# RG-LRU gates with the split halves stacked in rows, and a later start of the weight splits

## The chip, the cores and the metric

The kernel runs on one core of a Trainium2 chip. A core has a matrix engine (TensorE, PE in the profile), a vector engine (VectorE, DVE), a scalar engine (ScalarE, ACT), GpSimd (POOL), and SyncE (SP), whose queue issues the transfers. PE writes its products to banks of PSUM; ACT and DVE read them from there. All work in SBUF, a memory of 128 partitions (rows). The metric is the device time of one execution in microseconds; the median of three runs of the kernel before is 1309.77 us.

## The reference

One step of a two-layer encoder over 512 prompt tokens and 32 sample tokens, 544 columns in all, with 1024 features. Each layer projects its input to the parts of three branches: attention, retention, and a gated linear recurrence (RG-LRU). The branches are merged through gates, projected out, and normalised. What matters here is the third branch, 512 features wide:

```
xc = conv_b + sum(xpad[:, j:j + t] * conv_w[j] for j in range(CONV_W))
xb = xc.reshape(b, t, N_BLOCKS_C, BLOCK_C)
r = sigmoid(einsum('btni,nij->btnj', xb, w_gate_a) + b_gate_a)
ig = sigmoid(einsum('btni,nij->btnj', xb, w_gate_x) + b_gate_x)
log_a = -LRU_C * r * softplus(-lru_lambda);  a = exp(log_a)
bx = sqrt(-expm1(2.0 * log_a)) * ig * xc
```

then h[t] = a[t] h[t-1] + bx[t]. Both gate matrices are block diagonal: 8 blocks of 64 x 64.

## The kernel before

Features lie in partitions, 128 to a tile, tokens in columns. Every weight matrix is cut into blocks of 128 x 128 in the order of their use, eight to a chunk of 512 KB. A chunk is loaded by SP into one of three `raw` buffers. For products of nearly full precision each operand is split into a high part (rounded to the format fp32r, which PE multiplies in one pass) and a low part (the rest): for weights ACT casts the high part (L209) and DVE subtracts it to get the low part (L210), four blocks at a time, two in the first chunk. `hilo` (L261 to L263) does the same with activations. `block` (L254) multiplies one weight block in three products, high by high, high by low and low by high, each in two column ranges of 288 and 256: six instructions.

`layer_units()` lists a layer's work as units, each with one output tile: eight `pl` units of two blocks (the per-layer embedding, whose inputs are split by `ple_split`), then `xr`, `va`, `qa`, `ka` and so on, mostly of eight blocks. A unit accumulates in one of two `mm` buffers; afterwards `evac` copies the result out, for `pl` with an ACT copy (L931), for `xr` with two (L888, L889).

The order on each engine is the order in which the program writes the instructions down, under a manual schedule. `tick()` runs before each weight block. It first calls `stream()`, which splits weights until they are LEAD = 8 blocks ahead of the block in use, and asks for the next chunk when a chunk's second half is split. It then advances the waiting jobs, generators that give back after how many ticks they want to go on; PACE has these numbers. So a job's instructions stand at fixed places between PE's blocks, and each engine works its queue strictly in turn.

At the start PE runs WARM = 16 products of zeros (`busy`), `stream(2)` splits the first four blocks, `ple_split(0)` splits the first inputs, and the job `x_job` splits the residual stream from tick 5 on, one of eight tiles every two ticks.

The gates are the job `lru_tile(t)`, one for each of four feature tiles, added when `xr` unit t is out. ACT and DVE form the convolution `xc` over 547 columns (512 prompt tokens, 3 of convolution history, 32 sample tokens; L504, L506). After a pause the high and low part are made over 128 partitions. After another, and once for each of the two gates: a 128 x 128 weight block that holds two 64 x 64 blocks on its diagonal, zeros elsewhere, is multiplied in three products (high by high, high by low, low by high), in two overlapping column ranges of 274, into one of two `sc` banks and the one `pv` bank (L516). Three sigmoids with bias write the result to `lru_r` or `lru_i` (L519 to L521), leaving out the three history columns. Three ticks later comes the second gate, then two multiplies on POOL (L523, L524). The tiles 1 and 2 overlap in time, so their groups of products alternate. After the last tile `lru_job` computes the recurrence (exp, tanh, sqrt, scans).

The gate weights lie in a `held` buffer, eight blocks a layer (`wg`): four for one gate, four for the other.

Of the kernel before, what the change touches and what calls it, by code (L numbers as in the profile page):

```python
# [18 lines left out]
N = NP + NS  # L19
# [47 lines left out]
HELD = (6, 2)  # L67
WARM = 16

# [19 lines left out]
P_SC, P_SL = 52, 64  # L89
P_S0 = 68  # L90
NPAR = P_S0 + 256

# [31 lines left out]
def encoder(ctx: ExitStack, tc, xT, pT, W, RB, KC, VC, PAR, CST, LGB, o_y, o_k, o_v, o_rp, o_rs, o_cv, o_lr):  # L124
# [48 lines left out]
    def tick():  # L173
        clock[0] += 1
        stream()
        for j in list(jobs):
            while j[1] <= clock[0]:
                d = next(j[0], None)
                if d is None:
                    jobs.remove(j)  # L180
                    break
                j[1] = clock[0] + d
# [78 lines left out]
    def hilo(h, lo, src):  # L261
        S.copy(h, src)  # L262
        V.tensor_tensor(lo, src, h.bitcast(F32), SUB)  # L263
# [18 lines left out]
    def ple_split(l):  # L282
        pr, p2 = ple_in[l]
        for k in range(2):
            hilo(p2[:, k], p2[:, 2 + k], pr[:, k])

# [34 lines left out]
    def layer(l, env, nxt):  # L321
# [176 lines left out]
        def lru_tile(t):  # L498
            if t == 0:
                env["lru"] = [sl("lru_r"), sl("lru_i"), sl("lru_a")]  # L500
            R, I, _ = env["lru"]
            xrp = env["xrp"]
            xc = tmp("xc", (128, W547))
            S.activation(xc, xrp[:, t, 0:W547], AF.Identity, scale=pcol(P_CW, t), bias=pcol(P_CB, t))  # L504
            for j in range(1, 4):
                V.scalar_tensor_tensor(xc, xrp[:, t, j:j + W547], pcol(P_CW + 4 * j, t), xc, MUL, ADD)  # L506
            yield PACE["lt1"]
            xch, xcl = (tp_.tile([128, W547], F32R, tag="tmp", name="xch") for _ in range(2))
            hilo(xch, xcl, xc)
            yield PACE["lt2"]  # L510
            for g in range(2):
                w, lo = ([parts[(l * NB + AT["wg"] + g * 4 + t) // 4][i][:, t] for i in range(2)])
                ps = psum("sc"), psum("pv")
                for i, (wg, x) in enumerate(((w, xch), (w, xcl), (lo, xch))):
                    for p_, c0 in ((ps[0], 0), (ps[1], W547 - 274)):
                        T.matmul(p_[:, :274], lhsT=wg, rhs=x[:, c0:c0 + 274], start=i == 0, stop=i == 2)  # L516
                d = (I if g else R)[:, t]
                b_ = pcol(P_BX if g else P_BA, t)
                S.activation(d[:, :274], ps[0][:, :274], AF.Sigmoid, bias=b_)  # L519
                S.activation(d[:, 274:NP], ps[1][:, 1:NP - 273], AF.Sigmoid, bias=b_)  # L520
                S.activation(d[:, NP:], ps[1][:, 274 - NS:274], AF.Sigmoid, bias=b_)  # L521
                yield PACE["lt3"]
            G.tensor_tensor(I[:, t, :NP], I[:, t, :NP], xc[:, :NP], MUL)  # L523
            G.tensor_tensor(I[:, t, NP:], I[:, t, NP:], xc[:, NP + 3:], MUL)  # L524
            if t == 3:
                env["gates"] = True
                add(lru_job())

        def lru_job():
            R, I, A = env["lru"]  # L530

            for t in range(4):
                S.activation(A[:, t], R[:, t], AF.Exp, scale=sp[:, 1, l, t:t + 1])
                S.activation(R[:, t], R[:, t], AF.Tanh, scale=sp[:, 0, l, t:t + 1])
                yield PACE["lru0"]
            y = I
            for t in range(4):
# [8 lines left out]
            for t in range(4):  # L546
                G.tensor_tensor(R[:, t], R[:, t], I[:, t], MUL)
                yield PACE["lru3"]
                V.tensor_tensor_scan(y[:, t, :NP], A[:, t, :NP], R[:, t, :NP], 0.0, MUL, ADD)
                V.tensor_tensor_scan(y[:, t, NP:], A[:, t, NP:], R[:, t, NP:], pcol(P_SL, t), MUL, ADD)  # L550
            yield 2
# [487 lines left out]
    with tc.manual_schedule():  # L1039
        envs = [{} for _ in range(L + 1)]  # L1040
        stream(2)
        ple_split(0)
# [86 lines left out]
```

## Time and profile before

| | before |
|---|---|
| median of three runs | 1309.77 us (1309.71 to 1310.03) |
| the profiled execution | 1309.81 us, of which the span of the trace is 1308.0 us |
| instructions | 25456, of which PE 10744 products |
| transfers | 125.90 MB, mean 96 GB/s |
| granted TensorE clock | 0.997 |

In the page, a group's line has the source line, the engine, the operation, output and input by the program's names, their shapes, and how many there were; then busy time, mean duration in ns, and the idle time of the engine before them with its cause. A row of the timeline has the start, the length, engine, line, operation, names, shapes and count; in brackets stands idle time before it and who ended it. `sc`, `pv`, `tp` and `mm` are PSUM banks. Ends of products are modelled: products overlap in the pipeline, and their lengths don't add up to time.

### The profile page before, as it was taken

The page shows a single profiled execution, that of the slowest core. Times are in us where ns is not written, and L with a number is a line of the kernel's source. Part 1 is how long each engine was busy: PE and PEld are TensorE (multiplying, and loading weights), DVE is VectorE, ACT ScalarE, POOL GpSimd, SP SyncE. Part 2 cuts the span into 40 slices and gives each one's busy share as a digit, 9 for nine tenths or more (in the row PEclk, how much of TensorE's full clock was granted, in tenths as well). Part 3 has the DMA queues.
Part 4 walks back from the last instruction along what each step waited for, and adds up shares of the span by engine and source line. Part 5 has one row for each costly group of instructions (what it writes and reads, how often), then busy time and mean ns, then how long its engine had stood idle before and what let it go on. Part 6 is the DMA issues. An engine that isn't in the chain of part 4 may idle for free.

```text
span 1308.0 us, 25456 instructions
## 1 busy us (share of the span) xinstructions
PE 1291.7 (99%) x10744; PEld 1263.5 (97%) x10744; DVE 717.3 (55%) x1271; ACT 546.1 (42%) x1065; POOL 177.0 (14%) x158
## 2 busy tenths in 40 slices
PE   9999999999999999999999999999999999999996
PEld 9999999999999999999989998999999999999996
DVE  5666662573753453465584756626637444434567
ACT  6665544323632232333277655443235322332231
POOL 0210120410101201000032201224001011010000
PEclk9999999999999999999999999999999999999998
DMA  7233522231222222224112335222222222222231
GB/s 282 66 131 98 171 69 80 85 105 50 85 93 82 97 68 94 97 97 146 65 49 66 131 99 166 74 83 82 89 66 81 95 83 86 92 81 97 81 113 69
DMA packets 43457, 125.90 MB, mean 96 GB/s; under 512 B 9360, under 2 KB 11664, under 8 KB 42576
## 3 DMA queue, kind: packets, MB, share of 16 engines
q1 hardware_dynamic: 43344, 124.29, 28.8%
q8 instruction: 84, 1.38, 0.4%
q14 instruction: 29, 0.24, 0.1%
HBM read 112.57 MB, written 7.24 MB: 92 GB/s over the span
## 4 chain that ended last, share of the span: by engine, by line
PE 95%; DVE 3%; DMA 1%; ACT 1%; issue 0%; SPq 0%; POOL 0%; DVEq 0%
PE mm L254 84%; PE pv L432 2%; PE sc L402 2%; PE tp L418 1%; PE tp L330 1%; DMA raw<-in_W 1%; PE sc L661 1%; PE pv L684 1%; PE pv L516 0%; DVE r L813 0%; PE sc L516 0%; DVE xl L263 0%; PE sc L744 0%; PE sc L597 0%; PE pv L679 0%
## 5 line engine op out<-in xcount | busy, mean ns | idle before, releaser
L254 PE MATMUL mm<-xh,wh 128*128 128x288 f32 x2144 | 455.5, 294 | 0.4 <-ACT xrp L889 0.4
L254 PE MATMUL mm<-xh,wl 128*128 128x288 f32 x2144 | 444.1, 288 | 0.0
L254 PE MATMUL mm<-xl,wh 128*128 128x288 f32 x2144 | 442.7, 288 | 0.0
L210 DVE TENSOR_TENSOR wl<-raw,wh 128x512 fp32r<-128x512 f32 (+1 forms) x354 | 261.4, 756 | 283.8 <-ACT wh L209 279.9
L254 PEld LDWEIGHTS mm<-xh,wh 128*128 128x128 f32 x2144 | 328.3, 189 | 10.7 <-issue 7.4
L254 PEld LDWEIGHTS mm<-xl,wh 128*128 128x128 f32 x2144 | 328.8, 188 | 0.0
L254 PEld LDWEIGHTS mm<-xh,wl 128*128 128x128 f32 x2144 | 328.5, 188 | 0.2 <-DVE wl L210 0.2
L209 ACT CAST wh<-raw 128x512 fp32r<-128x512 f32 (+1 forms) x354 | 208.3, 614 | 36.9 <-PE mm L254 30.8
L911 ACT ACTIVATE sg<-mm 128x544 f32<-128x544 f32 x48 | 30.1, 626 | 154.1 <-PE mm L254 154.1
L923 POOL TENSOR_TENSOR m<-m,sg 128x544 f32<-128x544 f32 x30 | 46.8, 1560 | 316.6 <-DVE sg L921 316.6
L355 ACT ACTIVATE sx<-sx,sst 128x128 f32<-128x128 f32 (+4 forms) x68 | 38.0, 559 | 70.1 <-DVE sst L353 66.0
L254 PE MATMUL mm<-xh,held 128*128 128x288 f32 (+1 forms) x320 | 64.0, 291 | 0.3 <-ACT ple L931 0.3
L254 PE MATMUL mm<-ml,wh 128*128 128x288 f32 (+1 forms) x256 | 52.9, 288 | 0.0
L254 PE MATMUL mm<-mh,wl 128*128 128x288 f32 (+1 forms) x256 | 52.6, 286 | 0.0
L254 PE MATMUL mm<-mh,wh 128*128 128x288 f32 (+1 forms) x256 | 52.5, 286 | 0.0
L254 PEld LDWEIGHTS mm<-xh,held 128*128 128x128 f32 x320 | 51.3, 188 | 0.6 <-ACT ple L931 0.5
L254 PE MATMUL mm<-xl,held 128*128 128x288 f32 (+1 forms) x160 | 46.4, 290 | 0.5 <-DVE xl L263 0.5
L262 ACT CAST xh<-r 128x544 fp32r<-128x544 f32 (+2 forms) x32 | 17.0, 532 | 67.8 <-DVE r L938 63.6
L921 DVE TENSOR_TENSOR sg<-mm,sg 128x544 f32<-128x544 f32 x32 | 23.2, 725 | 36.7 <-PE mm L254 36.7
L565 POOL TENSOR_TENSOR swap<-swap,cst 128x544 f32<-128x544 f32 x16 | 25.3, 1580 | 109.8 <-DMA swap<-QB 68.1
L902 ACT ACTIVATE z<-mm 128x544 f32<-128x544 f32 x24 | 15.0, 626 | 59.2 <-PE mm L254 59.1
L254 PEld LDWEIGHTS mm<-mh,wl 128*128 128x128 f32 x256 | 39.3, 188 | 0.0
(251 smaller groups left out, 1791.9 us busy)
## 6 DMA issues: line engine op xcount, KB each, us to landing
raw<-in_W SPq DMA_DIRECT2D x189, 512.0 KB, 3.3
bias<-in_RB SPq DMA_DIRECT2D x16, 256.0 KB, 4.1
x<-in_xT SPq DMA_DIRECT2D x4, 544.0 KB, 9.2
o_v<-VA SPq DMA_DIRECT2D x2, 1088.0 KB, 5.1
o_k<-KT SPq DMA_DIRECT2D x2, 1088.0 KB, 5.1
swap<-KB SPq DMA_DIRECT2D x32, 68.0 KB, 2.0
swap<-QB SPq DMA_DIRECT2D x32, 68.0 KB, 2.0
o_y<-tk SPq DMA_DIRECT2D x6, 256.0 KB, 2.1
```

The lines of the kernel that those rows point to most:

```text
L209: S.copy(h[:, k:k + step], t)
L210: V.tensor_tensor(lo[:, k:k + step], t, h[:, k:k + step].bitcast(F32), SUB)
L254: T.matmul(ps[:, MM0 + a:MM0 + b], lhsT=w[:, n % 4, :], rhs=x[:, a:b], start=first and i == 0, stop=last and i == 2)
L262: S.copy(h, src)
L355: S.activation(x, x, AF.Exp, bias=s[:, 0:1], scale=-1.0, accum_out=s[:, 1:2])
L402: T.matmul(scs[j][:, o:o + n], lhsT=q_[r, p, i * 128:i * 128 + 128], rhs=k_[r, p, :n], start=k == 0, stop=k == 2)
L432: T.matmul(pv[64 * j:64 * j + 64, i * 128:i * 128 + 128], lhsT=env["vatok"][:, kt, h * 64:h * 64 + 64], rhs=xs[j][:, o:o + 128], start=kt ...
L565: G.tensor_tensor(sw, sw, cst[:, C_SIN:C_SIN + N], MUL)
L902: S.activation(z, pv, AF.Sigmoid)
L911: S.activation(sg, pv, AF.Sigmoid)
L921: V.tensor_tensor(sg, pv, sg, MUL)
L923: (V if kind == "bB" and t == 7 else G).tensor_tensor(m, m, sg, ADD)
```

## The change

The gates: for each half b of a tile (64 features) one operand `xs[b]` now holds the high part in that half's own 64 rows and the low part in the other 64 rows. The weight block for half b is the half's two 64 x 64 matrices side by side (gate a and gate x in the columns, in the other order for the second half), repeated in the upper and lower rows. One product with the block's high part gives high by high plus high by low for both gates, one with its low part gives the rest, now with low by low. So a half takes two products in two column ranges, a tile 8 instructions and not 12. The high part is cast by two ACT instructions of 64 rows, and the low part by two DVE subtractions that write to the other 64 rows. Each half's result is read by four sigmoids of 64 rows (two gates, two column ranges), which write all 547 columns; a shifted copy of one bias (`P_BXS`) is added to the parameters. `lru_r`, `lru_i` and `lru_a` get 547 columns, POOL multiplies once, and the scans of the sample tokens start three columns later in their inputs.

The start: in the first eight ticks `stream` keeps 2 blocks ahead, not 8; the first `ple_split` works its first tile in the two column ranges of the products; WARM is 14. The first call is `stream(1)`, which like `stream(2)` splits the first four blocks.

```
-WARM = 16
+WARM = 14
     def tick():
         clock[0] += 1
-        stream()
+        stream(LEAD if clock[0] > 8 else 2)
     def ple_split(l):
         for k in range(2):
-            hilo(p2[:, k], p2[:, 2 + k], pr[:, k])
+            for a, b in SPANS if l == 0 and k == 0 else ((0, N),):
+                hilo(p2[:, k, a:b], p2[:, 2 + k, a:b], pr[:, k, a:b])
         def lru_tile(t):
-                env["lru"] = [sl("lru_r"), sl("lru_i"), sl("lru_a")]
+                env["lru"] = [sl(k, shape=(128, 4, W547)) for k in ("lru_r", "lru_i", "lru_a")]
-            xch, xcl = (tp_.tile([128, W547], F32R, tag="tmp", name="xch") for _ in range(2))
-            hilo(xch, xcl, xc)
+            xs = [tp_.tile([128, W547], F32R, tag="tmp", name="xhl") for _ in range(2)]
+            rows = slice(0, 64), slice(64, 128)
+            for b in range(2):
+                S.copy(xs[b][rows[b]], xc[rows[b]])
+            for b in range(2):
+                V.tensor_tensor(xs[b][rows[1 - b]], xc[rows[b]], xs[b][rows[b]].bitcast(F32), SUB)
             yield PACE["lt2"]
-            for g in range(2):
-                w, lo = ([parts[(l * NB + AT["wg"] + g * 4 + t) // 4][i][:, t] for i in range(2)])
+            for b in range(2):
+                n = l * NB + AT["wg"] + 2 * t + b
                 ps = psum("sc"), psum("pv")
-                for i, (wg, x) in enumerate(((w, xch), (w, xcl), (lo, xch))):
+                for i in range(2):
                     for p_, c0 in ((ps[0], 0), (ps[1], W547 - 274)):
-                        T.matmul(p_[:, :274], lhsT=wg, rhs=x[:, c0:c0 + 274], start=i == 0, stop=i == 2)
-                d = (I if g else R)[:, t]
-                b_ = pcol(P_BX if g else P_BA, t)
-                S.activation(d[:, :274], ps[0][:, :274], AF.Sigmoid, bias=b_)
-                S.activation(d[:, 274:NP], ps[1][:, 1:NP - 273], AF.Sigmoid, bias=b_)
-                S.activation(d[:, NP:], ps[1][:, 274 - NS:274], AF.Sigmoid, bias=b_)
+                        T.matmul(p_[:, :274], lhsT=parts[n // 4][i][:, n % 4], rhs=xs[b][:, c0:c0 + 274],
+                                 start=i == 0, stop=i == 1)
+                for d, r, b_ in ((R, rows[b], P_BA), (I, rows[1 - b], P_BXS)):
+                    b_ = pcol(b_, t)[r]
+                    S.activation(d[rows[b], t, :274], ps[0][r, :274], AF.Sigmoid, bias=b_)
+                    S.activation(d[rows[b], t, 274:], ps[1][r, 1:274], AF.Sigmoid, bias=b_)
                 yield PACE["lt3"]
-            G.tensor_tensor(I[:, t, :NP], I[:, t, :NP], xc[:, :NP], MUL)
-            G.tensor_tensor(I[:, t, NP:], I[:, t, NP:], xc[:, NP + 3:], MUL)
+            G.tensor_tensor(I[:, t], I[:, t], xc, MUL)
         def lru_job():
-            y = I
+            y = I[:, :, :N]
-                V.tensor_tensor_scan(y[:, t, NP:], A[:, t, NP:], R[:, t, NP:], pcol(P_SL, t), MUL, ADD)
+                V.tensor_tensor_scan(y[:, t, NP:], A[:, t, NP + 3:], R[:, t, NP + 3:], pcol(P_SL, t), MUL, ADD)
-        stream(2)
+        stream(1)
             if kind == "wg":
-                W[l, n // 8, :, n % 8] = 0
-                for b in range(2):
-                    r = slice(64 * b, 64 * b + 64)
-                    W[l, n // 8, r, n % 8, r] = g["w_gate_x" if k // 4 else "w_gate_a"][l, 2 * (k % 4) + b]
+                ax = [g[a][l, k] for a in ("w_gate_a", "w_gate_x")]
+                W[l, n // 8, :, n % 8] = np.tile(np.concatenate(ax[::-1] if k % 2 else ax, 1), (2, 1))
```

More of the change, by code (lines that the diff above doesn't have):

```diff
@@ L89 @@
 P_SC, P_SL = 52, 64
-P_S0 = 68
+P_BXS = 68
+P_S0 = 72
 NPAR = P_S0 + 256
@@ L1094 @@
             put(c, feat(g[k][l], t))
+        put(P_BXS, np.roll(feat(g["b_gate_x"][l], 4), 64, 0))
         put(P_SC, feat(g["state_conv"][l, 0], 4))
```

## The prediction

> **What bounds the kernel now.** I read the page first, then the matrix engine's (PE's) instructions around the gate products, then the scalar engine (ACT) in the same stretch, and last the first 20 us.
>
> ```profile
> PE 1291.7 (99%) x10744; PEld 1263.5 (97%) x10744; DVE 717.3 (55%) x1271; ACT 546.1 (42%) x1065; POOL 177.0 (14%) x158
> ...
> PE 95%; DVE 3%; DMA 1%; ACT 1%; issue 0%; SPq 0%; POOL 0%; DVEq 0%
> ```
>
> PE sets the end almost everywhere, so a product that disappears shortens the run unless PE then waits. The gate products are a small part of it (all instructions that touch the split convolution result):
>
> ```profile
> L516 PE MATMUL sc<-xch,held x48: 283/288/295, 42.3 to 710.9; 128*128 128x274 f32 x48
> ```
>
> 48 of these go to the `sc` banks, and as many to `pv`. Now PE in layer 1's gate stage, one instruction to a row (start, length):
>
> ```profile
> 690.33 0.29 PE L516 MATMUL sc<-xch,held 128*128 128x274 f32 x1
> ...
> 690.58 0.29 PE L516 MATMUL sc<-xch,held 128*128 128x274 f32 x1
> ...
> 691.10 0.41 PE L254 MATMUL mm<-xh,wh 128*128 128x288 f32 x2
> ...
> 698.65 0.29 PE L516 MATMUL sc<-xch,held 128*128 128x274 f32 x1
> ...
> 700.18 0.29 PE L516 MATMUL sc<-xch,held 128*128 128x274 f32 x1
> 700.56 0.39 PE L516 MATMUL pv<-xch,held 128*128 128x274 f32 x1
> 700.79 0.28 PE L516 MATMUL sc<-xch,held 128*128 128x274 f32 x1
> ```
>
> Six products take 691.10 - 690.33 = 0.77, so one costs 0.128 us of PE; its 0.29 is mostly pipeline. The reader is to see the gap at 700.18: the next product should follow at 700.31 and starts at 700.56. PE stood 0.25 us although the page calls it busy, because the ends of products are modelled. What it waited for is in ACT's list:
>
> ```profile
> 691.17 0.49 ACT L519 ACTIVATE lru_r<-sc,par 128x274 f32<-128x274 f32 x1 [2.17 <-PE sc L516]
> 691.56 0.45 ACT L520 ACTIVATE lru_r<-pv,par 128x238 f32<-128x238 f32 x1
> 691.90 0.29 ACT L521 ACTIVATE lru_r<-pv,par 128x32 f32<-128x32 f32 x1
> 692.07 0.66 ACT L262 CAST xch<-xc 128x547 fp32r<-128x547 f32 x1
> 692.80 0.59 ACT L888 COPY xrp<-mm 128x512 f32<-128x512 f32 x1
> ...
> 693.36 0.63 ACT L209 CAST wh<-raw 128x512 fp32r<-128x512 f32 x1
> 694.19 0.49 ACT L519 ACTIVATE lru_i<-sc,par 128x274 f32<-128x274 f32 x1 [0.20 <-PE sc L516]
> ...
> 695.09 0.66 ACT L262 CAST xch<-xc 128x547 fp32r<-128x547 f32 x1
> 695.63 0.86 ACT L504 ACTIVATE xc<-xrp,par 128x547 f32<-128x547 f32 x1
> 696.38 0.62 ACT L209 CAST wh<-raw 128x512 fp32r<-128x512 f32 x1
> 697.21 0.49 ACT L519 ACTIVATE lru_r<-sc,par 128x274 f32<-128x274 f32 x1 [0.21 <-PE sc L516]
> ...
> 699.49 0.49 ACT L519 ACTIVATE lru_r<-sc,par 128x274 f32<-128x274 f32 x1 [1.26 <-PE sc L516]
> ...
> 700.22 0.29 ACT L521 ACTIVATE lru_r<-pv,par 128x32 f32<-128x32 f32 x1
> 701.37 0.49 ACT L519 ACTIVATE lru_i<-sc,par 128x274 f32<-128x274 f32 x1 [0.86 <-PE sc L516]
> ...
> 702.27 0.62 ACT L855 COPY VA<-mm 128x544 f32<-128x544 f32 x1
> ...
> 703.65 0.49 ACT L519 ACTIVATE lru_i<-sc,par 128x274 f32<-128x274 f32 x1 [0.23 <-PE sc L516]
> ...
> 711.21 0.49 ACT L519 ACTIVATE lru_i<-sc,par 128x274 f32<-128x274 f32 x1 [0.26 <-PE sc L516]
> ```
>
> There is one `pv` bank. The last read of it ends at 700.22 + 0.29 = 700.51, and PE's `pv` product starts at 700.56. Tiles 1 and 2 run interleaved, one unit of work apart. From 691.17 to 697.21 ACT has only 0.20 and 0.21 us to spare: there the change puts its new work.
>
> **The change in the gates.** Per tile and layer it takes 4 of 12 products off PE: 32 x 0.128 = 4.1 us in all. What comes in their place:
>
> ACT. A group's evacuation was three sigmoids that occupy it for 692.07 - 691.17 = 0.90 us. It becomes four, each of 274 or 273 columns on 64 rows. No row has 64 rows of this; bounds: 0.39 (691.17 to 691.56, the same columns on 128 rows) if the columns count, half of that if the elements do. I take 0.39, because the rows of 274, 238 and 32 columns already differ by columns. So 1.56 us for ACT, and 3 x 0.39 + 0.49 = 1.66 until the bank is read out, 1.71 with the 0.05 to PE's start. The cast of the split (0.54, 695.09 to 695.63) becomes two on 64 rows: 1.08.
>
> The Trainium skill's page "ScalarE: Activation LUTs", section "What ACT_TABLE_LOAD costs", speaks against the change here: an activation with a per-partition bias costs a fixed part and a part per column, about 280 + 0.833 N ns, 93 ns of it overlapped back to back, and rows do not enter. That would be an estimated 0.415 us for each instead of the trace's 0.39, and would make the total about 0.9 us longer than mine; the trace's row decides.
>
> VectorE (DVE) gets a second subtraction of 0.7 us a tile (1.2 when GpSimd, POOL, runs). POOL gets one multiply instead of two. The scans keep their lengths, and other operations become three columns wider. All that lies beside PE's stream; the weight splits have eight blocks of lead, 8 x 0.75 = 6 us (a block is six products of L254), against an ACT delay that stays below 2 us below.
>
> Now ACT's queue, in its order, for layer 1; b0 and b1 are a tile's two halves. A group of four products occupies PE for 0.51, and its first sigmoid can start 0.25 + 0.33 = 0.59 after the group (690.58 is 0.25 after 690.33; the last `sc` product to sigmoid takes 0.33). PE's old group starts are the sigmoid's start less 0.84 (691.17 - 690.33).
>
> - Tile 0 b0: PE 690.33, ACT 690.92 to 692.48. Casts 1.08 to 693.56, xrp 0.56 (692.80 to 693.36), weight cast 0.52: 694.65.
> - Tile 0 b1: PE 693.10, ready at 693.69, but ACT comes at 694.65; `pv` free at 696.36. ACT then has casts, xc (0.75) and a weight cast: 698.56.
> - Tile 1 b0: PE at 695.86, its `pv` product due at 695.99 waits 0.37; group done at 696.36 + 0.49 = 696.85 (a product that waited holds PE 0.23, 700.56 to 700.79). ACT reads at 698.56: `pv` free at 700.27.
> - Tile 2 b0: two blocks later, due at 698.50, waits 1.77; done at 700.76. ACT is ready with it, 700.83; free at 702.54.
> - Tile 1 b1: one block later, due at 701.64, waits 0.90; done at 703.03; free at 704.81. ACT then copies VA and casts a weight, 1.02.
> - Tile 2 b1: two blocks later, due at 704.67, waits 0.14; done at 705.30. Before, it ended at 703.65 - 0.84 + 0.77 = 703.58.
> - Tile 3: its cast follows at 707.2, and its subtraction beside POOL:
>
> ```profile
> 705.24 1.21 DVE L263 TENSOR_TENSOR xch<-xc,xch 128x547 fp32r<-128x547 f32 x1 [1.10 <-ACT xch L262]
> ```
>
> so its first product can start at 709.2, 0.12 after PE would be there (five blocks, 3.76, after 705.30). Its second group ends at 712.48; before, at 711.21 - 0.84 + 0.77 = 711.14.
>
> So layer 1 becomes 1.3 us longer: 2.05 saved, and 0.25 of old waiting gone, against 3.3 of waiting and 0.4 of restarts. Layer 0 has the same order, with a table load that I estimate to cost 0.1 more: 1.4. Together **+2.7 us**. Bounds: -4.6 if ACT keeps pace (4.1 and two old waits), +7.2 if each of the sigmoids takes its whole 0.49 (rival B).
>
> **The change at the start.**
>
> ```profile
> 3.76 0.71 ACT L209 CAST wh<-raw 128x256 fp32r<-128x256 f32 x2 [1.54 <-DMA raw<-in_W]
> 4.59 1.30 ACT L262 CAST phl<-pr 128x544 fp32r<-128x544 f32 x2
> 7.62 0.71 ACT L209 CAST wh<-raw 128x256 fp32r<-128x256 f32 x2 [1.74 <-DMA raw<-in_W]
> ...
> 9.40 1.12 ACT L931 COPY ple<-mm 128x544 f32<-128x544 f32 x2
> ...
> 13.87 0.63 ACT L209 CAST wh<-raw 128x512 fp32r<-128x512 f32 x1
> 14.39 0.65 ACT L262 CAST xh<-x 128x544 fp32r<-128x544 f32 x1
> ...
> 19.39 0.61 ACT L931 COPY ple<-mm 128x544 f32<-128x544 f32 x1 [0.28 <-PE mm L254]
> ```
> ```profile
> 1.20 4.00 PE L269 MATMUL mm<-zero 128*128 128x272 f32 x16 [1.20 <-DVE eps L289]
> ...
> 5.29 1.52 PE L254 MATMUL mm<-phl,wh 128*128 128x288 f32 x4
> ...
> 10.05 0.77 PE L254 MATMUL mm<-phl,wh 128*128 128x288 f32 x4 [0.71 <-ACT ple L931]
> ```
> ```profile
> 3.07 0.43 SPq L297 DMA_DIRECT2D x<-in_xT  x1
> ```
> ```profile
> x<-in_xT SPq DMA_DIRECT2D x1, 544.0 KB, 7.1
> ```
>
> PE waits until 10.05 for the first output copy (9.40), which stood in ACT's queue behind weight casts that waited for transfers (7.62 and the one after it). With two blocks of lead in the first ticks the copy comes first. Splitting the first cast lets PE begin about 0.2 us earlier (a 288-column piece, 0.43, after 4.59); I take the first unit as done that much sooner, 7.3 instead of about 7.6. The copy then runs at 7.6, the casts at 8.1, and the third unit starts at 8.8, not 10.05. But the x casts now stand ahead of later output copies. The first x transfer is issued at 3.07 and lands 7.1 later, 10.2: x cast, output copy, weight cast (0.55, 0.50, 0.52) end at 11.9 where PE wanted that weight at 11.8, and its low part comes 0.7 later: 0.3 us of waiting. From there ACT is the slower one again; its last copy of this stage comes at 18.5 instead of 19.39. **-0.9 us**; bounds: -1.3 (all of the 10.05 start kept), 0 (ACT's work is the same, only its order differs). Two warm-up products less lie before the first real one and move nothing. The load after the second weight chunk is asked for some 2 us later, since that chunk is split later; its products are in the gate stage at 42 us, so that is covered.
>
> **Sum.** 1309.81 (the profiled execution; span 1308.0 and 1.8 around it, 0.04 above the median shown) + 1.3 + 1.4 - 0.9 = **1311.6 us**, +0.14%. A measurement tells 0.2% (2.6 us) from no change, so this is no change, close to the slower side.
>
> **Rivals.**
> A, ACT keeps pace: 64 rows cost half, or the bank is free earlier. Then only the savings stay: 1309.8 - 4.6 - 0.9 = 1304.3. For it: 0.86 and 1.26 us of ACT idle time before 701.37 and 699.49. Against it: none ahead of 697.21, and the delay arises there.
> B, slower, the evacuation of `pv` decides wholly: the four sigmoids, reading the same two banks by turns, do not overlap, 0.49 each. The same queue then gives waits of 1.1, 2.2, 1.2 and 0.4, and 0.6 at tile 3, and so 3.5 and 3.7 more in the two layers: 1309.8 + 7.2 - 0.9 = 1316.1. It decides as soon as an evacuation and what stands ahead of it exceed the 1.5 us between groups. Against it: 0.39 from 691.17 to 691.56 although two banks are read.
> C, the start gives nothing or costs: the x cast holds ACT, or the clock rises later. The 16 warm-up products take 4.00 us, 0.25 each against 0.13 later; if the gap that opens before the first real product made PE go through such a slow stretch again, half of 4 us is lost. So 1312.5 (gain of nothing) to 1314.5 (2 lost). The Trainium skill's "TensorE: Matmul & The Clock Gate", "What's actually happening", has a free-running window of about 3.4 us; by it the half-microsecond gap alone changes nothing, but the moment varies between executions.
>
> **Chances.** Forecast 0.55, with its own range 1309.5 to 1313.3 (0.45 of it within 0.2%, 0.10 above); A 0.18; B 0.12; C 0.15, of which 0.10 is slower. So faster 0.18, within 0.2% 0.50, slower 0.32. The range for eight in ten takes in A's value and the upper part of C, and leaves out B: 1304.3 to 1314.3.
>
> **What would show it.** The queue is right if the third group (tile 2 b0) has its `pv` product over 1.5 us behind its `sc` one, with a sigmoid just ended, in both layers. A holds if that gap is below 0.3. The sigmoids' starts, 0.39 or 0.49 or 0.2 apart, decide between all three. At the start: the third unit near 8.8, and PE's block after the last copy near 19.1 instead of 20.05. The forecast is wrong if the evacuations don't line up in that order, or if a later stage, whose bound I leave alone, takes up the difference.

## The result, and the profile after

The changed kernel takes **1318.04 us** (median of 6 runs, 1317.05 to 1321.20) against 1309.91 for the kernel before on the same chip: a ratio of 1.0065, with a 95% interval of 1.0052 to 1.0078. It is slower, by 8 us, where 1311.6 was forecast with 1314.3 as the upper end. The profiled execution took 1317.05 us with a span of 1315.3.

All the kernels below have the same 9024 products in `block`, in the same order. So the start of the n-th one in two traces can be subtracted. "Late" below means this difference against the kernel before, in us; negative is early. For the changed kernel:

| the product that the kernel before starts at | 41.5, before layer 0's gates | 64.6, behind them | 689.3, before layer 1's gates | 712.6, behind them | 796.4, in layer 1's attention | the last one |
|---|---|---|---|---|---|---|
| late | -1.1 | 3.1 | 3.0 | 6.2 | 7.0 | 7.3 |

In this execution the start gained what it was to gain. Each gate stage lost: 4.2 us in layer 0, 3.2 in layer 1. The rest, 0.8, was lost in layer 1's attention stage. From the page of the changed kernel, busy times and the chain of work that ended last:

```profile
PE 1290.8 (98%) x10710; PEld 1260.6 (96%) x10710; DVE 724.6 (55%) x1280; ACT 564.3 (43%) x1090; POOL 169.6 (13%) x150
...
PE 90%; DVE 5%; ACT 3%; issue 1%; DMA 1%; SPq 0%; POOL 0%; DVEq 0%; ACTq 0%
```

PE has 34 instructions less (32 gate products, 2 warm-ups), ACT 25 more and 18 us more to do; ACT's share of the chain rose from 1% to 3%, DVE's from 3% to 5%. PE's waits (total, count, longest) have a new first line:

```profile
PE pv L525 <- ACT lru_i L531: 7.9, 6, 1.9
```

PE in layer 1's gates, the groups that answer to the prediction's third to sixth:

```profile
698.85 0.28 PE L525 MATMUL sc<-xhl,held 128*128 128x274 f32 x1
700.14 0.39 PE L525 MATMUL pv<-xhl,held 128*128 128x274 f32 x1 [1.00 <-ACT lru_i L531]
...
702.17 0.39 PE L525 MATMUL sc<-xhl,held 128*128 128x274 f32 x1
704.51 0.39 PE L525 MATMUL pv<-xhl,held 128*128 128x274 f32 x1 [1.94 <-ACT lru_i L531]
...
705.75 0.28 PE L525 MATMUL sc<-xhl,held 128*128 128x274 f32 x1
706.86 0.39 PE L525 MATMUL pv<-xhl,held 128*128 128x274 f32 x1 [0.82 <-ACT lru_i L531]
...
708.86 0.29 PE L525 MATMUL sc<-xhl,held 128*128 128x274 f32 x1
709.20 0.40 PE L525 MATMUL pv<-xhl,held 128*128 128x274 f32 x1
```

A `pv` product is due 0.13 behind its `sc` product, so the waits are 1.16, 2.21, 0.98 and 0.21. The prediction had 0.37, 1.77, 0.90 and 0.14. In layer 0 the same four are 1.56, 2.21, 0.98 and 0.04. So the sign that the prediction named, a third group whose `pv` product stands over 1.5 us behind its `sc` one, is there in both layers. And ACT in layer 1's stretch:

```profile
693.90 0.49 ACT L530 ACTIVATE lru_r<-sc,par 64x274 f32<-64x274 f32 x1 [1.12 <-PE sc L525]
694.29 0.47 ACT L531 ACTIVATE lru_r<-pv,par 64x273 f32<-64x273 f32 x1
694.78 0.49 ACT L530 ACTIVATE lru_i<-sc,par 64x274 f32<-64x274 f32 x1
695.17 0.47 ACT L531 ACTIVATE lru_i<-pv,par 64x273 f32<-64x273 f32 x1
695.66 1.32 ACT L516 CAST xhl<-xc 64x547 fp32r<-64x547 f32 x2
697.01 0.59 ACT L897 COPY xrp<-mm 128x512 f32<-128x512 f32 x1
...
697.71 0.62 ACT L211 CAST wh<-raw 128x512 fp32r<-128x512 f32 x1
698.36 0.49 ACT L530 ACTIVATE lru_r<-sc,par 64x274 f32<-64x274 f32 x1
```

Look at the distances of the starts. The first two sigmoids work on the same 64 rows, and the second starts 0.39 behind the first. The third works on the other rows and starts 0.49 behind the second; the cast, 0.49 behind the fourth. So an evacuation takes 695.66 - 693.90 = 1.76, not 1.56, and two casts 697.01 - 695.66 = 1.35, not 1.08. The Trainium skill's "ScalarE: Activation LUTs", section "What ACT_TABLE_LOAD costs", lets back-to-back activations overlap by about 93 ns: that agrees where the rows stay (0.49 - 0.39 = 0.10), and does not where they change.

### The profile page after: what moved, and what is told of

It is laid out like the page before. It is cut to its first block, busy times and chain, and to the rows that moved or that the text cites. A ratio compares the mean times of both kernels' runs of the same rounds, so it can differ in the third digit from the quotient of the medians.

```text
span 1315.3 us, 25413 instructions
## 1 busy us (share of the span) xinstructions
PE 1290.8 (98%) x10710; PEld 1260.6 (96%) x10710; DVE 724.6 (55%) x1280; ACT 564.3 (43%) x1090; POOL 169.6 (13%) x150
## 4 chain that ended last, share of the span: by engine, by line
PE 90%; DVE 5%; ACT 3%; issue 1%; DMA 1%; SPq 0%; POOL 0%; DVEq 0%; ACTq 0%
PE mm L256 80%; PE pv L436 2%; PE sc L406 1%; PE tp L422 1%; PE tp L334 1%; PE sc L670 1%; PE pv L693 1%; DVE wl L212 1%; DVE r L822 0%; ACT xhl L516 0%; DVE xl L265 0%; PE sc L753 0%; PE sc L606 0%; DVE xc L510 0%; PE pv L688 0%
## 5 line engine op out<-in xcount | busy, mean ns | idle before, releaser
L256 PEld LDWEIGHTS mm<-mh,wh 128*128 128x128 f32 x256 | 39.1, 188 | 0.0
```

The source lines that it names most:

```text
L256: T.matmul(ps[:, MM0 + a:MM0 + b], lhsT=w[:, n % 4, :], rhs=x[:, a:b], start=first and i == 0, stop=last and i == 2)
```

## The experiments

In the tables, "late" is as above: at the product of 41.5 us, of 64.6, 117.1 (layer 0's attention), 689.3, 712.6, and the last. Ratios are against the kernel before on the same chip.

### The two parts of the change, each by itself

`e1_start_only` is the kernel before with the start of the changed one; `e2_gates_only` the changed kernel with the old start.

```
e1, in before:                       e2, in after:
-WARM = 16                           -WARM = 14
+WARM = 14                           +WARM = 16
-stream()                            -stream(LEAD if clock[0] > 8 else 2)
+stream(LEAD if clock[0] > 8 else 2) +stream()
...                                  ...
```

> The kernel before with the changed start alone (lead of two blocks in the first eight ticks, first input split in two pieces, 14 warm-up products). Theory, the start gains and keeps it: in the changed kernel the product that follows the last pl copy starts at 18.99 us and not 20.06, so 1309.9 - 1.1 = 1308.8 us. Rival, the gain is given back when ACT or a transfer is late further on: 1309.9 us.

> The changed kernel with the start of before. Theory, all of the loss is in the gate stages: 1318.0 + 1.1 = 1319 us, with the same products in `pv` waiting 1 to 2.2 us. Rival, the new start is part of the loss (ACT begins the gate stage later): 1310 to 1316 us.

| | us | ratio | late |
|---|---|---|---|
| e1_start_only | 1309.17 (1308.63 to 1311.03) | 0.9997 (0.9989 to 1.0006) | -0.7, -0.7, -0.7, -0.8, -0.8, -0.8 |
| e2_gates_only | 1318.76 (1317.33 to 1319.40) | 1.0064 (1.0048 to 1.0079) | -0.2, 5.0, 5.0, 4.9, 8.4, 9.4 |

The whole loss comes with the change of the gates: without the new start, e2 loses 5.2 and 3.5 us in the gate stages and 1.0 in layer 1's attention. In e1's profiled execution the start gains 0.8 us; over 11 runs that can't be told from nothing.

### Is it the bank, or ACT's work?

Two rivals of the explanation "ACT has too much to do": the order in which the banks are read, and the single `pv` bank. `e3_pv_first` reads the `pv` bank's two halves ahead of the `sc` bank's, so `pv` is free sooner. `e4_two_banks` lets the second half of the columns go to `pv` and `tp` by turns.

```
e3: -for d, r, b_ in (gate a, gate x):  sc, pv
    +for bank in (pv, sc):  gate a, gate x
e4: -ps = psum("sc"), psum("pv")
    +env["turn"] = 1 - env.get("turn", 0)
    +ps = psum("sc"), psum("pv" if env["turn"] else "tp")
```

> The changed kernel, but the two sigmoids that read `pv` come before the two that read `sc`, so that the one `pv` bank is free after two sigmoids (about 0.9 us) and not after four (1.75). Theory, ACT as a whole is late and the bank only passes it on: the first wait falls from 1.2 to about 0.4, the second stays near 2, the third falls to 0.4; 1.1 to 1.8 us gained a layer, so 1315 to 1316 us. Rival, the single bank alone is the bound: every wait shrinks by 0.85 or to nothing, some 3.5 to 4 us a layer with the restarts, 1310 to 1311 us.

> The changed kernel, but the groups take the `pv` and the `tp` bank by turns, so that a group no longer needs the bank of the group before it. Theory, ACT has 17 us of work where PE leaves it 11.5: two of the waits go and new ones come at the third tile's end (2 us at tile 1 b1, 1.7 before tile 3, which waits for its cast), 1.6 us gained a layer: 1314 to 1315.5 us. Rival, the bank alone: no waits, 1304 to 1305 us.

| | us | ratio | late |
|---|---|---|---|
| e3_pv_first | 1318.90 (1317.89 to 1320.62) | 1.0070 (1.0056 to 1.0083) | 2.7, 6.7, 6.7, 6.6, 10.3, 10.8 |
| e4_two_banks | 1317.18 (1316.99 to 1318.61) | 1.0058 (1.0044 to 1.0071) | 0.1, 4.0, 4.0, 3.9, 7.5, 8.8 |

Neither gave what either theory expected. The bank alone is refuted: with two of them the gates lose 3.9 and 3.6 us all the same. PE's first wait in e4 is another one:

```profile
PE sc L526 <- DVE xhl L518: 6.6, 4, 1.9
```

PE now waits for the split, and the split for ACT: tile 3's cast stands in ACT's queue behind sixteen sigmoids, a copy and a weight cast, without a gap.

```profile
703.63 0.48 ACT L531 ACTIVATE lru_r<-sc,par 64x274 f32<-64x274 f32 x1
...
711.83 1.32 ACT L516 CAST xhl<-xc 64x547 fp32r<-64x547 f32 x2
```

And e3's order costs something of its own. ACT in e3:

```profile
697.59 0.49 ACT L532 ACTIVATE lru_r<-pv,par 64x273 f32<-64x273 f32 x1 [1.26 <-PE pv L525]
698.09 0.49 ACT L532 ACTIVATE lru_i<-pv,par 64x273 f32<-64x273 f32 x1
698.60 0.49 ACT L534 ACTIVATE lru_r<-sc,par 64x274 f32<-64x274 f32 x1
699.10 0.49 ACT L534 ACTIVATE lru_i<-sc,par 64x274 f32<-64x274 f32 x1
699.62 1.32 ACT L516 CAST xhl<-xc 64x547 fp32r<-64x547 f32 x2
```

Now each sigmoid has other rows than the one before, and all four are 0.50 apart, also the second and the fourth, which stay in their bank: it is the rows that decide, and not the bank.

### ACT's work alone, in the kernel before

`e5_before_casts` only casts the high part in two halves of 64 rows; `e6_before_sigmoids` only splits the two larger sigmoids of each gate into halves of 64 rows. The products stay as before.

```
e5: -hilo(xch, xcl, xc)
    +for r in (slice(0, 64), slice(64, 128)):
    +    S.copy(xch[r], xc[r])
    +V.tensor_tensor(xcl, xc, xch.bitcast(F32), SUB)
e6: +for r in (slice(0, 64), slice(64, 128)):
         S.activation(d[r, :274], ps[0][r, :274], ...)
         S.activation(d[r, 274:NP], ps[1][r, 1:NP - 273], ...)
```

> The kernel before, with only the cast of the convolution's high part split into two casts of 64 rows each. No product changes. Theory, two ACT operations on different rows don't overlap (0.67 us from start to start in the changed kernel, not 0.55): 0.8 us more ACT work a tile, which makes tile 2's first `pv` product wait about 0.7 us: +0.7 a layer, 1311.3 us. If they overlap as operations on 128 rows do, 0.55 more a tile and +0.2 a layer, 1310.3 us. Rival, ACT work does not matter and the new products are slow: 1309.9 us.

> The kernel before, with only the sigmoids of 274 and 238 columns split into two of 64 rows each (five instead of three; an evacuation takes about 1.85 us of ACT and not 0.90). No product changes. Theory, ACT work ahead of the `pv` bank makes the loss: waits of about 1.4, 1.0, 0.3 and 0.6 us a layer, +3.1 a layer, so about 1316 us, without a single new product. Rival, the stacked operands or the products are at fault: under 1311 us.

| | us | ratio | late |
|---|---|---|---|
| e5_before_casts | 1311.00 (1310.42 to 1311.42) | 1.0008 (0.9998 to 1.0017) | -0.2, 0.3, 0.3, 0.7, 1.2, 1.2 |
| e6_before_sigmoids | 1316.14 (1315.73 to 1316.39) | 1.0045 (1.0031 to 1.0058) | -0.4, 2.7, 2.7, 2.7, 5.9, 5.9 |

e6 came as expected. e5 lies between the two values of its theory, nearer to the higher one, but its interval takes in no change, so it shows little by itself. Not one product is changed in e6, and it loses 3.2 us in each gate stage. ACT's rows, and PE's first wait:

```profile
693.82 0.48 ACT L520 ACTIVATE lru_r<-sc,par 64x274 f32<-64x274 f32 x1 [2.17 <-PE sc L516]
694.21 0.44 ACT L521 ACTIVATE lru_r<-pv,par 64x238 f32<-64x238 f32 x1
694.66 0.48 ACT L520 ACTIVATE lru_r<-sc,par 64x274 f32<-64x274 f32 x1
```
```profile
PE pv L516 <- ACT lru_r L522: 4.4, 4, 1.1
```

A sigmoid of 64 rows takes as long as one of 128 (0.39 to the next), and the 238 columns take 0.45 to a neighbour with other rows, where the kernel before had 0.34 (691.56 to 691.90) to one with the same rows. The same difference again, 0.11. All of these write to `lru_r`, so the change from `lru_r` to `lru_i`, which goes along with the change of rows in the other runs, isn't the reason either.

### What are the removed products worth?

`e13_eight` is the kernel before with the third product of each gate group left out (the gates get less exact), and nothing else changed.

```
-for i, (wg, x) in enumerate(((w, xch), (w, xcl), (lo, xch))):
+for i, (wg, x) in enumerate(((w, xch), (w, xcl))):
```

> The kernel before with the third product of each gate group left out (the weights' low part by the features' high part), so that 8 products a tile remain and nothing else changes; this leaves a part of the computation out, the gates are a little less exact. Theory 1 (the products are worth what the sum took for them, 2.05 us a layer and 0.25 of old waiting): 1305.2. Theory 2 (the attention stage is bound by DVE's chain, 0.4 us behind PE in the kernel before, and takes back what PE comes early): PE is 2 us early after the gates and about 0.5 us early after the attention stage's start in each layer, 1308.5 to 1309.

1306.31 us (1305.95 to 1306.86), ratio 0.9971 (0.9960 to 0.9983). Late: 0.0, -2.1, -2.1, -2.2, -4.3, -3.0. So the products were worth 2.1 us a layer, as the sum had it, and layer 0's attention stage takes nothing back. In layer 1's 1.2 us are lost, and the old wait for `pv`, which the theory had gone, stays at 0.25 us in each layer. Together that is the 1.7 us by which the profiled execution, 1306.86, lies above the 1305.2 of the first theory. In layer 1's attention stage DVE waits for POOL, which writes into a bias that was loaded:

```profile
742.93 0.29 DVE L353 CUSTOM_DVE_ANT_0 sx<-sc,bias 128x128 f32<-128x128 f32 x1 [1.37 <-POOL bias L373]
```

The changed kernel has the same row with a wait of 0.98, and POOL in it waits for the transfer:

```profile
753.57 0.14 POOL L377 MEMSET bias<- 64x64 f32 x1 [0.57 <-DMA bias<-in_RB]
```

That fits the 0.8 us that its attention stage lost, which come in one step, at 758.8 us of its trace. When this transfer lands was not varied, so the cause is argued here, not shown.

### Taking ACT's work away

Five runs give ACT more room. `e7_spread` puts the groups further apart in time (five ticks); `e8_spread_dve` four ticks, with the casts on DVE and e3's order; `e10_tight` three ticks with casts on DVE and e4's two banks; `e11_short` is e8 with the recurrence's steps closer together; `e14_relief` has the casts on DVE and the two banks, and no group is moved.

```
e7:  -"lt3": 3                          +"lt3": 5
     -yield PACE["lt1"]                 +yield PACE["lt1"] + (0, 4, 12, 14)[t]
e8:  "lt3": 4, (0, 2, 8, 8)[t], and
     -S.copy(xs[b][rows[b]], xc[rows[b]])
     +V.tensor_copy(xs[b][rows[b]], xc[rows[b]])
e10: (0, 0, 4, 2)[t], V.tensor_copy, e4's banks
e11: e8 with "lru0", "lru1" and "lru3" at 2 instead of 3
e14: V.tensor_copy, e4's banks
```

> The changed kernel with the groups of gate products spread over more of PE's other work: five ticks between two groups and no two tiles interleaved. Nothing else differs. Theory, the products saved are worth what was worked out, and only ACT's lateness takes it back: no `pv` wait over 0.3 us, 1309.9 - 4.6 - 1.1 = 1304.2 us, faster than the kernel before. Rival, the stacked products or the extra DVE and ACT work cost by themselves: 1312 us or more.

> The changed kernel with four ticks between groups, no two tiles interleaved, the `pv` sigmoids first, and the two 64-row casts on VectorE instead of ACT. Theory as for five ticks: no waits, 1304.2 us; a little less waiting later in the layer, since the recurrence starts 5 us earlier than with five ticks. If VectorE, which is busy with the convolution there, becomes the bound, the casts come late: 1305 to 1308 us.

> The changed kernel with its two casts on DVE, the second bank of a group alternating between pv and tp, and the groups evenly spaced, three ticks apart, so that the last group comes two ticks later than in the kernel before. Theory (ACT had some 17 us of work where PE left it 11.5; here DVE takes 2.7 us a tile from it and the groups leave it 2.8 to 3 us each against a need of about 3.1 that the second bank absorbs): the gate waits are below 0.5 us a layer, the savings of 2 us a layer and the start stay, and two ticks of delay do not reach the attention stage: 1304 to 1305. Rival 1 (any delay of the recurrence runs into the attention stage's norm): 1306 to 1310. Rival 2 (another reason than ACT's work makes the gates slow): 1315 to 1317.

> The run with spread groups and casts on DVE, in which the gate waits were gone but 5 us a layer were lost when the attention stage began, with the recurrence's steps put two ticks apart instead of three, so that it ends as early as in the kernel before. Theory (that loss came from the recurrence's DVE and ACT work, 8 us late, running beside the attention's first norm): the loss goes and the time is 1304 to 1306. Rival (the loss has another source, or the recurrence packed closer takes as much of DVE there): 1312 to 1316.

> The changed kernel with its two casts on DVE and the second bank of a group alternating between pv and tp; groups and recurrence stay in their ticks. Theory (ACT's work, 17 us where PE leaves 11.5, makes the waits; without 4 us of casts and with a second bank they are below 0.5 us a layer): PE is 1.5 to 2 us early after each gate stage. If the attention stage takes nothing back: 1305 to 1306; if it takes back all but 0.5 us a layer: 1307.5 to 1308.5. Rival (the waits come from another source): 1314 to 1317.

| | us | ratio | late |
|---|---|---|---|
| e7_spread | 1329.04 (1328.55 to 1329.92) | 1.0144 (1.0130 to 1.0158) | -0.7, -4.0, 8.9, 9.0, 5.3, 18.7 |
| e8_spread_dve | 1314.90 (1314.74 to 1316.05) | 1.0038 (1.0025 to 1.0051) | -1.0, -4.0, 2.5, 2.3, -1.2, 5.1 |
| e10_tight | 1316.26 (1315.58 to 1318.75) | 1.0054 (1.0040 to 1.0068) | -0.7, 1.2, 3.1, 2.9, 2.1, 6.4 |
| e11_short | 1317.38 (1316.44 to 1318.88) | 1.0060 (1.0047 to 1.0073) | -0.1, -3.1, 4.0, 4.0, 0.6, 7.6 |
| e14_relief | 1310.32 (1308.39 to 1311.45) | 1.0003 (0.9994 to 1.0011) | -0.8, -0.6, -0.6, -0.8, -1.5, -1.5 |

All five missed the times of their theories. (e10 lies in the range of its second rival, but with another wait, given below.) In e7, e8 and e11 PE comes out of layer 0's gates 3.0 to 3.3 us earlier than it went in; the waits for `pv` are gone. (Part of that is only put off, since tile 3's products stand behind 64.6 there.) By 117.1, in the attention stage, 6 to 13 us are lost. PE's first wait in e8, and the row in e11:

```profile
PE tp L422 <- DVE sx L364: 5.5, 4, 2.5
```
```profile
104.58 0.90 PE L422 MATMUL tp<-cst,sx 128*128 128x128 f32 x3 [2.88 <-DVE sx L364]
```

The recurrence, which starts when the last group is out, now runs into the first softmax: both need DVE, which works its queue in order. To end it as early as before, as in e11, isn't enough. In the kernel before, the softmax comes ahead of the third scan; in e11 it comes behind it, 3.9 us later. DVE in the two:

```profile
97.71 0.28 DVE L353 CUSTOM_DVE_ANT_0 sx<-sc,bias 128x128 f32<-128x128 f32 x1
...
98.26 1.22 DVE L549 TENSOR_TENSOR_SCAN lru_i<-lru_a,lru_r 128x512 f32<-128x512 f32 x1
```
```profile
99.22 1.22 DVE L561 TENSOR_TENSOR_SCAN lru_i<-lru_a,lru_r 128x512 f32<-128x512 f32 x1
100.36 1.33 DVE L562 TENSOR_TENSOR_SCAN lru_i<-lru_a,par,lru_r 128x32 f32<-128x32 f32 x1
101.61 0.26 DVE L357 CUSTOM_DVE_ANT_0 sx<-sc,bias 128x128 f32<-128x128 f32 x1
```

e10 loses 1.9 and 4.2 us there, and 1.9 in layer 0's gates, where it has the wait that e14 shows. e14, which leaves every group in its tick, loses nothing in the attention stages. Its rival is refuted: no `pv` wait is left in PE's list. What remains is a wait on DVE, before tile 2's first group:

```profile
51.42 0.36 PE L526 MATMUL sc<-xhl,held 128*128 128x274 f32 x1 [1.85 <-DVE xhl L518]
```
```profile
47.95 1.75 DVE L212 TENSOR_TENSOR wl<-raw,wh 128x512 fp32r<-128x512 f32 x1
49.62 0.90 DVE L516 CAST xhl<-xc 64x547 fp32r<-64x547 f32 x2
50.55 1.48 DVE L518 TENSOR_TENSOR xhl<-xc,xhl 64x547 fp32r<-64x547 f32 x2
```

The casts that left ACT stand in DVE's queue, and tile 2's split ends at 52.0, behind a weight split of 1.75 (0.69 otherwise), while its first half alone is wanted at 49.6. In layer 1 it is the casts that are slow, 2.08 for the two instead of 0.90. These two waits, 1.9 and 1.2 us in PE's list, are most of the 3.7 us by which e14's gate stages gain less than e13's. They don't explain that e14's median lies 1.9 us above its profiled execution (1308.39). `e15_relief_early` (e14 with "lru0" and "lru1" at 2) tested whether an earlier recurrence helps.

> As e14_relief, with the recurrence's first two steps two ticks apart instead of three, so that it ends up to eight ticks earlier. Theory (the attention stage waits for DVE because the recurrence's scans stand ahead of its first norm): the attention stage takes nothing back, 1304.5 to 1305.5, and 2 us less than e14_relief if that one loses there. Rival (ACT or DVE is full in that stretch whatever the order): as e14_relief or slower, 1308 to 1312.

1320.74 us (1320.33 to 1323.39), ratio 1.0085 (1.0071 to 1.0099). Late: 1.4, 1.7, 8.1, 7.9, 7.2, 12.9. Its theory fell, and its rival was too mild: the recurrence's steps, closer together, make a weight split and a copy late at 89 and 91 us, 1.9 us each.

### The version that beats both

`e16_halves` puts the split's four DVE operations in the order cast, subtraction, cast, subtraction. It also moves tile 2's split one tick earlier, which its expectation doesn't name; in its trace ACT's order in the gate stages is that of e14, and DVE's too but for these operations. `e17_halves_early` moves tile 2's split two ticks earlier, ahead of the weight split. The products stay where they were in both.

```
e16, in e14:  for b in range(2):
                  V.tensor_copy(xs[b][rows[b]], xc[rows[b]])
             -for b in range(2):
                  V.tensor_tensor(xs[b][rows[1 - b]], ...)
             -yield PACE["lt1"]                 +yield PACE["lt1"] - 1 * (t == 2)
             -yield PACE["lt2"]                 +yield PACE["lt2"] + 1 * (t == 2)
e17, in e16: -yield PACE["lt1"] - 1 * (t == 2)  +yield PACE["lt1"] - 2 * (t == 2)
             -yield PACE["lt2"] + 1 * (t == 2)  +yield PACE["lt2"] + 2 * (t == 2)
```

> As e14_relief, with the split's four DVE operations in the order cast, subtraction, cast, subtraction, so that a tile's first half is ready before its second is begun. Theory (PE waits 1.9 us in each layer for tile 2's first half alone): the half is ready 0.6 us earlier, at about 50.8 on e14's time line, PE waits 1.2, and the time is about 1.2 us below e14_relief: 1308.8 to 1309.4. Rival (the wait is for both halves or moves on to the next group): as e14_relief, 1310.3.

> As e16_halves, with tile 2's split two ticks earlier, ahead of a weight split in DVE's queue; the products stay where they are. Theory: tile 2's first half starts at about 47.95 instead of 49.62 and is ready between 49.2 and 50.3 (the later if GpSimd's multiply slows the subtraction by 1.1 us), where PE is due at 49.6; the waits are at most 0.7 us, and the time is 2.4 to 3.7 us below e14_relief: 1306.6 to 1307.9. Rival 1 (the weight split that stands behind it now is late for its product): 1309 to 1311. Rival 2 (the attention stage takes back what the gates gain): 1308.5 to 1309.5.

| | us | ratio | late |
|---|---|---|---|
| e16_halves | 1307.93 (1307.24 to 1310.43) | 0.9989 (0.9981 to 0.9998) | 1.3, 0.9, 0.9, 0.7, -0.6, -0.1 |
| e17_halves_early | 1306.64 (1306.03 to 1308.53) | 0.9978 (0.9969 to 0.9987) | -1.0, -2.0, -2.0, -2.1, -4.3, -3.9 |

e16's median gained twice what was expected of it, which its profiled execution, one with a late start, does not explain. Nor does that execution bear out its theory: in layer 0 PE still waits 1.80 us for tile 2's first half (1.85 in e14), with tile 1's second subtraction, 1.78 us long, ahead of it in DVE's queue. e17 is 3.3 us faster than the kernel before, within the times of its theory, and 11 us faster than the change, with the change's products. DVE and PE in it, layer 0:

```profile
47.03 1.79 DVE L517 TENSOR_TENSOR xhl<-xc,xhl 64x547 fp32r<-64x547 f32 x1
...
49.30 0.72 DVE L517 TENSOR_TENSOR xhl<-xc,xhl 64x547 fp32r<-64x547 f32 x1
```
```profile
50.17 0.37 PE L525 MATMUL sc<-xhl,held 128*128 128x274 f32 x1 [1.18 <-DVE xhl L517]
```

In layer 0 1.2 us of waiting are left, 0.5 more than expected: it is now tile 1's subtraction that is slow, 1.79 instead of 0.72. In layer 1 there is no such wait, and the gates gain 2.1 us.

### The clock, and the start

`e9_fill` puts products of zeros, which nothing reads, into PE's waits for `pv`. `e12_warm` is e1 with 16 warm-up products.

```
e9, between sc and pv:  +if tile 1 or tile 2 b0:
                        +    for _ in range(12 if t == 2 else 6):
                        +        T.matmul(fill[:, :H2], lhsT=zero[:, :128], rhs=zero, start=True, stop=True)
e12, in e1:  -WARM = 14   +WARM = 16
```

> The changed kernel with products of zeros, whose result nothing reads, put into a bank that is free at that time, between the sc and the pv products of tile 1 b0 (6 of them), tile 2 b0 (12) and tile 1 b1 (6); nothing else changes. Theory (the short waits themselves are 2 to 5 us a layer, and on top of them they let PE's clock fall, which cost about 1.0 us in layer 0 of the profiled run): the products lie in the waits, 6 x 0.13 = 0.8 us in a wait of 1.2 and 12 x 0.13 = 1.6 in one of 2.2, the granted clock stays at 1.00 through both gate stages, and the time is 1316.0 to 1316.5 with less than 0.7 us between the runs. Rival (the clock has nothing to do with the waits): as the changed kernel, 1317 to 1321, or above it by what the products cost.

> The change of the start alone, with 16 products of zeros ahead of the first real product instead of 14. Theory (with 14 a gap opens before the first real product, in which the clock falls in some executions, which spread the start-only runs from 1308.6 to 1311.0): the spread shrinks below 1 us and the median is 1308.5 to 1308.9. Rival (whether the clock falls is chance, whatever stands there): the same spread, 1308.6 to 1311, and a median of 1309.2.

| | us | ratio | late |
|---|---|---|---|
| e9_fill | 1318.46 (1317.42 to 1320.34) | 1.0066 (1.0054 to 1.0079) | -0.1, 3.4, 4.4, 5.4, 8.6, 8.6 |
| e12_warm | 1309.28 (1308.71 to 1310.02) | 0.9995 (0.9987 to 1.0004) | -0.8, -0.8, -0.8, -0.9, -0.9, -0.9 |

In the changed kernel's layer 0, two-microsecond windows of PE (length, busy time and count, granted clock, DMA share, GB/s) show the clock at half behind the waits; e9's show it whole, with PE kept busy:

```profile
50.00:52.00 2.00, 0.84 (x6) 1.00 0.00 0
52.00:54.00 2.00, 1.21 (x9) 1.00 0.06 8
54.00:56.00 2.00, 1.18 (x7) 0.82 0.32 78
56.00:58.00 2.00, 2.00 (x11) 0.50 0.46 184
58.00:60.00 2.00, 2.00 (x15) 0.82 0.00 0
```
```profile
54.00:56.00 2.00, 1.98 (x16) 1.00 0.00 0
56.00:58.00 2.00, 1.95 (x15) 1.00 0.70 262
```

From 41.5 to 64.6 e9 lost 3.5 us where the changed kernel lost 4.2; in layer 1, where the clock stayed whole in both, it lost the same 3.2. So within these two profiles the fill does its part, 0.6 of the 1.0 expected. The granted clock agrees in every run: 0.997 or 0.998 in e9's five, 0.992 to 0.996 in the changed kernel's six. So with the waits filled the clock stays up. But the time of the runs is no lower, and their spread is 2.9 us where it was to be below 0.7 (4.2 in the changed kernel): e9's profile was 0.9 less early after the start, lost 1.0 in layer 0's attention stage, and 1.0 at 601 us, where a weight cast came late. The expected times are missed, and e9's slowest run, 1320.34 us at a clock of 0.997, shows that the clock isn't all that spreads the runs. e12's runs spread by 1.3 us where e1's did by 2.4, which was to be below 1, with no lower median: inconclusive.

## Why the prediction was wrong

**The step that failed** is ACT's price in "the change in the gates": "I take 0.39 ... So 1.56 us for ACT" and, for the casts, "1.08". Measured were 1.76 and 1.35. The two bounds named there (0.39 and half of it) left out that neighbours on different rows do not overlap; the copy and the weight cast behind the casts took longer here too (697.01 to 697.71 is 0.70 for `xrp`, and 0.65 to 698.36, against 0.56 and 0.52). The 0.65 is such a change again: the sigmoid behind this weight cast reads rows 64 to 127, and a weight cast ahead of one on rows 0 to 63 took 0.50 (702.22 to 702.72). Why `xrp` took 0.70 stays open.

**The queue was right.** The same steps with the measured prices: tile 0 b0 from 690.92, evacuation 1.76, casts 1.35, 0.70 and 0.65, so that b1 is read from 695.38 and `pv` is free at 697.15 (0.39 + 0.48 + 0.39 + 0.47 + 0.04 on). Tile 1 b0, due at 695.99, waits 1.16: measured 1.16. ACT comes to it at 699.75, `pv` is free at 701.52; tile 2 b0, due two blocks behind 697.64, waits 2.24: measured 2.21. Small differences add up, because ACT had no room from one group to the next: 0.20 of the first evacuation, 0.27 of its casts, 0.27 of the two operations behind them and 0.05 of the second evacuation are the 0.79 by which tile 1 b0 waits longer.

**Layer by layer.** Layer 1: 1.3 predicted, 3.2 measured, of which 1.6 is in the five waits (4.9 instead of 3.3, tile 3's 0.36 among them). The other 0.3 isn't accounted for. Layer 0: 1.4 predicted, 4.2 measured, 1.0 more than layer 1. Its waits sum to no more than layer 1's (4.8), so the 1.0 lies elsewhere: the stretch of half clock stands there, which the prediction did not have in the gates, and with the waits filled, in e9, the stretch was gone and layer 0 lost 0.6 less. The attention stage of layer 1: 0 predicted, 0.8 measured; the forecast named such a later stage as what would prove it wrong. With the start's 0.2 the other way that is 1.9 + 2.8 + 0.8 - 0.2 = 5.3 of the 5.45 us between 1311.6 and the profiled 1317.05. The median lies 1.0 higher still: the runs lie from 1317.05 with a granted clock of 0.996 to 1321.20 with 0.992.

**The products**: 4.1 us predicted, 4.1 measured in e13. **The start**: third unit predicted near 8.8, the block behind the last copy near 19.1:

```profile
8.86 0.67 PE L256 MATMUL mm<-phl,wh 128*128 128x288 f32 x4
...
18.99 0.51 PE L256 MATMUL mm<-xh,wh 128*128 128x288 f32 x2
```

Right in this execution; but in those of e15 and e16 rival C's slower clock came. That the gap ahead of the first real product brings it on is not shown. Of 14 profiled kernels with the new start, eight were 0.7 to 1.1 us early at 41.5, three within 0.2 of before, and three were 1.3 to 2.7 late, as e16 here:

```profile
6.00:8.00 2.00, 1.24 (x6) 0.88 0.97 351
8.00:10.00 2.00, 2.00 (x10) 0.50 1.01 401
```

**The rivals.** A fell: ACT doesn't keep pace. B had the waits nearly as they came (1.1, 2.2, 1.2, 0.4, 0.6 against 1.16, 2.21, 0.98, 0.21, 0.36) and 1316.1 us, with the mechanism half right: sigmoids do not overlap, but at a change of rows and not at a change of banks. That its waits came so near is partly luck: it priced an evacuation at 1.96 us, 0.20 too much, and left the casts and what stands behind them as they were, 0.54 too little. B was argued away with the 0.39 from 691.17 to 691.56, a pair with two banks and the same rows, and so was left out of the range. The estimate of 0.415 for each sigmoid from the Trainium skill's "ScalarE: Activation LUTs", "What ACT_TABLE_LOAD costs", lies between my 0.39 and the measured mean of 0.44.

## What to carry to other kernels

Work cut into halves of the rows costs the scalar engine twice the instructions at full price, and a little more at every change of rows; count that against the matrix products it saves, along the queue and not as a mean over the kernel. Where the trace has no row for a shape, keep its dearest neighbour within the range if the engine has no room between two deadlines. And when work moves between engines, leave the stages in their places: the runs that moved the groups gave back at the next stage more than the gates had gained.

## What the runs showed of the hardware

- ACT: neighbouring operations overlapped by 0.10 us when they worked on the same rows, and not when the next one worked on the other 64 rows: 0.39 against 0.49 to 0.50 from start to start with 273 or 274 columns, 0.34 against 0.45 with 238. From a weight cast of all 128 rows to a sigmoid there was overlap where the sigmoid reads rows 0 to 63 (0.50), and none where it reads rows 64 to 127 (0.65); so it may be the first row that counts, which no run tested by itself. Two casts of 64 rows and 547 columns take 1.35 together, one of 128 rows 0.54.
- PE's clock fell to half behind waits of at most 2.2 us each, with PE busy 3.2 of the 6 us from 50 to 56. The slow stretch, from about 55.3 to 58.7, lasted 3.4 us. That agrees with the window of about 3.4 us in the Trainium skill's "TensorE: Matmul & The Clock Gate", section "What's actually happening"; but its condition, an idle window of that length, wasn't met here: PE had products in between. The section "A second HAM failure mode: psum-queue depth-cycling" of the Trainium skill's same page, on short idles between groups, fits better. The slow stretch isn't certain to come: layer 1 of the same execution, with such waits and PE busy 3.2 of the 6 us from 702 to 708, kept the full clock, and so did e6, busy 3.8 of the 6 us from 50 to 56.
- DVE's operations of 0.7 us took 1.7 to 1.8 in some rows of e14 and e17, which moved the deadline by 1 us. POOL's multiply ran beside each of these: from 46.77 to 48.23 beside e17's 1.79. In e17's trace the 292 such subtractions (weights of 512 columns, the split) that no POOL instruction touched in time took at most 0.73 us, and the 33 that took longer all lay beside one; but 41 others beside POOL stayed short. What POOL runs there was not varied.
